# A hybrid diffusion backbone on one core: TensorE's instructions kept in the order of the source

## The chip, the cores and the metric

The kernel runs on one core of one Trainium2 chip. The metric is device time in microseconds (us), median of three runs. The engines of the core are TensorE (PE, matmuls and transposes; its weight loads are shown apart as PEld), VectorE (DVE), ScalarE (ACT), GpSimd (POOL) and SyncE (SP), which issues most DMA transfers. Every engine works through its own list of instructions in order and waits at the head of the list for semaphores of the others.

## The reference, cut to what matters

Two layers (DEPTH = 2) run over 1024 latent tokens and 128 context tokens, width 1024. Each layer has a modulated RMSNorm, three groups of mixers that share one input and one output projection, and a squared-ReLU MLP:

```python
h = rmsnorm(x, p['norm_mix_pre']) * (1 + scale1) + shift1
proj = h @ p['w_in']
o_a = block_attention(qa, k_all, v_all, HEAD_DIM ** -0.5)              # 6 heads, 2 of keys
o_b = block_attention(q_b, k_b, kv[..., B_NOPE:], (B_NOPE + B_ROPE) ** -0.5)  # 4 heads, low rank
o_c, h_fin = ssd_mixer(z, xbc, dt_raw, p, h0)                          # state-space scan, both ways
x = x + gate1 * rmsnorm(concatenate([o_a, o_b, o_c]) @ p['w_out'], p['norm_mix_post'])
h = rmsnorm(x, p['norm_ffn_pre']) * (1 + scale2) + shift2
f = square(relu(h @ p['w_ffn1'])) @ p['w_ffn2']
x = x + gate2 * rmsnorm(f, p['norm_ffn_post'])
```

Softmax in block_attention is over all 1152 keys for latent queries and over the 128 context keys for context queries.

## The kernel before, in words

The 1152 tokens are nine tiles of 128, or three blocks of 384 (`NB = 3`). A product in full precision is made of three matmuls: operands are split into a rounded part (ACT, `cp`) and the rest (DVE or POOL, `lo`). Stages follow each other for each layer: `in_proj` (input projection, convolution, and the scan's first half `ssm_a`), `mix` (keys and values, attention, the scan's second half `ssm_b`, output projection), `ffn` (MLP), whose last part overlaps the next layer's start.

The program is written as one list of calls in Python. Side work is written as generators that stand in a list `self.bg`. At fixed places of the main work the source calls `self.pull(ns)`, which steps the generators, so that their instructions land among those of the main work; a generator can yield a number of nanoseconds for which it wants to be left alone (`D`), and `PU` holds what each place in the main work counts for. So the source has an order of its own, written out by hand. A scheduler then builds the list of each engine: it takes the instructions by their order in the source as priority, runs a timeline of its own, and lets a later instruction go first when the earlier one's inputs or buffers are not there yet. It does so for all five engines.

Attention works on groups, one head of one block of 384 queries: 12 groups with the low-rank keys, then 18 with the others, a layer. For a group `score` makes scores S (PE), copies them to P with a running maximum (DVE, L777), and after the third piece of a row of 128 queries takes the exponential of the row of 1152 (ACT). `trans` transposes P (PE, tile pt), and splits it into ph (ACT) and pl (DVE); `prod` multiplies with the values (PE, tile oT). The main loop issues this for each of nine pieces of 128 keys, with the scores of the next group between:

```python
            ts = [trans(g, 0), trans(g, 1)]
            for j in range(nj):
                if j + 2 < nj:
                    ts.append(trans(g, j + 2))
                if nx and j < 9:
                    score(nx, j // 3, j % 3)
                prod(g, j, ts[j])
```

Three more places matter. `o_split` transposes attention's output (PE, tile m) into the operands of `out_proj` (PE, tile op, 8 x 24 matmuls a block); for the last block that is issued after attention, together with the norms `prenorm` of the first two blocks. A norm has two steps on PE (`stats`): sums over the partitions (tile st), then, after a short chain on DVE and POOL, a broadcast of the factors (tile rb). `chain` in `ffn` runs two such norms a block while the MLP ends. The start of the kernel does the same for the three blocks of the input.

Of the kernel before, what the change touches and what calls it, by code (L numbers as in the profile page):

```python
# [30 lines left out]
class Group:  # L31

    def __init__(self, b, prep, V, scale, dst, done, pull, after=None):
        self.b, self.prep, self.V, self.scale, self.dst, self.done = b, prep, V, scale, dst, done
        self.pull, self.after = pull, after


class Net:
    def __init__(self, tc, a, o):
        self.tc, self.nc, self.a, self.o = tc, tc.nc, a, o  # L40
        self.bg = []
        self.used = [0.0, 0.0, 0.0]
        self.credit = self.now = self.hold = 0.0
        self.build()


    def pool(self, name, side="left", space=None, bufs=1):
# [1575 lines left out]
```

## Time and profile before

| | |
|---|---|
| median of 3 runs | 3482.16 us (3480.79 to 3486.63) |
| profiled execution, its own time | 3485.52 us |
| its span, first to last instruction | 3483.7 us |
| mean granted clock of TensorE | 0.963 |
| PE, DVE, ACT, POOL busy | 93%, 65%, 45%, 39% |

Busy is the share of the span in which the engine had an instruction under way. PE's matmuls are pipelined, each of them overlaps the next, so its busy time is not time at its peak. [...]

### The profile page before, as it was taken

Reading aid. Unit: us, or ns where it says so; the run is one execution under the profiler, and the core shown is the slowest. Engines: PE = TensorE matmul, PEld = TensorE weight load, DVE = VectorE, ACT = ScalarE, POOL = GpSimd, SP = SyncE. Lnnn points to the kernel's source line nnn. Section 1 sums busy time; section 2 is a strip of 40 time slices with the busy share of each in tenths; the row PEclk is TensorE's granted clock in tenths of the full one; section 3 lists DMA queues with packets and bytes.
Section 4 is the critical chain, followed back from the end, with each engine's and each line's share of the span. In section 5 each row is a group of like instructions: output and inputs, shape, how many; then the busy total and the mean of one; then the engine's idle time right before and its main releaser. Section 6 shows DMA issues by size and latency. Waiting matters only on the chain. (4 is left out here: it accounts for less than half of the span.)

```text
span 3483.7 us, 50649 instructions
## 1 busy us (share of the span) xinstructions
PE 3234.2 (93%) x18578; PEld 3055.2 (88%) x18578; DVE 2257.0 (65%) x5318; ACT 1557.5 (45%) x3250; POOL 1348.8 (39%) x996
## 2 busy tenths in 40 slices
PE   6988799998899999999989887999888999999997
PEld 3966698788799999999989676989887999999997
DVE  6876888765647778774588767887658223333236
ACT  4464677665441221112454646787654411222223
POOL 6357432144651122113573673331356412111145
PEclk8989899999999999999999998999998999999999
DMA  5253333413332333322432533322233211111134
GB/s 212 80 175 104 115 86 116 164 49 97 126 103 80 94 99 98 91 91 73 145 120 97 170 112 111 89 92 67 79 108 98 85 37 45 41 43 43 37 97 145
DMA packets 164525, 340.71 MB, mean 98 GB/s; under 512 B 14429, under 2 KB 105909, under 8 KB 160693
## 3 DMA queue, kind: packets, MB, share of 16 engines
q1 hardware_dynamic: 161012, 335.32, 30.2%
q8 instruction: 146, 2.39, 0.3%
q10 hardware_dynamic: 3264, 2.16, 0.2%
q14 instruction: 103, 0.84, 0.1%
HBM read 280.99 MB, written 56.44 MB: 97 GB/s over the span
## 5 line engine op out<-in xcount | busy, mean ns | idle before, releaser
L78 POOL TENSOR_TENSOR w<-raw,w 128x1024 fp32r<-128x1024 f32 (+1 forms) x266 | 650.6, 2451 | 1370.8 <-ACT w L65 1314.8
L69 PE MATMUL g<-h,w 128*128 128x384 f32 x5328 | 971.5, 342 | 10.5 <-DVE h L78 6.4
L69 PEld LDWEIGHTS g<-h,w 128*128 128x128 f32 x5328 | 949.5, 190 | 16.5 <-DVE h L78 8.6
L69 PE MATMUL g<-big,w 128*128 128x384 f32 x4608 | 818.7, 336 | 8.4 <-DVE big L78 3.4
L69 PEld LDWEIGHTS g<-big,w 128*128 128x128 f32 x4608 | 802.5, 189 | 12.4 <-DVE big L78 5.2
L65 ACT CAST w<-raw 128x1024 fp32r<-128x1024 f32 (+1 forms) x266 | 275.9, 1042 | 643.5 <-PE g L69 353.1
L83 DVE TENSOR_TENSOR big<-big,g 128x384 f32<-128x384 f32 x336 | 181.8, 550 | 289.4 <-PE g L69 289.1
L83 DVE TENSOR_TENSOR r<-r 128x384 f32<-128x384 f32 x192 | 148.5, 773 | 329.0 <-ACT r L97 328.4
L69 PE MATMUL g<-w,h 128*128 128x512 f32 (+1 forms) x1296 | 321.6, 402 | 31.1 <-ACT w L65 12.2
L777 DVE TENSOR_SCALAR_CACHE_REDUCE P<-S 128x384 f32<-128x384 f32 (+1 forms) x500 | 265.8, 541 | 112.3 <-PE S L69 108.3
L69 PEld LDWEIGHTS g<-w,h 128*128 128x128 f32 x1296 | 252.7, 199 | 77.4 <-ACT w L65 13.5
L78 DVE TENSOR_TENSOR pl<-pt,ph 128x384 fp32r<-128x384 f32 (+2 forms) x560 | 267.7, 498 | 43.4 <-ACT ph L65 39.7
L65 ACT CAST ph<-pt 128x384 fp32r<-128x384 f32 (+2 forms) x560 | 232.2, 445 | 84.4 <-PE pt L73 72.1
L93 DVE SCALAR_TENSOR_TENSOR macc<-raw,cT,macc 128x128 f32<-128x128 f32 x784 | 259.9, 393 | 0.0
L73 PE MATMUL pt<-cst,P 128*128 128x128 f32 x1460 | 257.9, 276 | 0.5 <-DVE pl L78 0.3
L97 ACT ACTIVATE r<-g 128x384 f32<-128x384 f32 x192 | 94.2, 491 | 355.2 <-PE g L69 354.9
L78 DVE TENSOR_TENSOR big<-r,big 128x384 fp32r<-128x384 f32 x192 | 172.3, 897 | 92.6 <-ACT big L65 92.4
L69 PE MATMUL op<-big,w 128*128 128x384 f32 x1152 | 227.3, 340 | 2.0 <-DVE big L78 1.6
L97 ACT ACTIVATE P<-P,mx 128x1152 f32<-128x1152 f32 x180 | 210.4, 1170 | 37.0 <-DVE mx L89 36.0
L69 PEld LDWEIGHTS op<-big,w 128*128 128x128 f32 x1152 | 199.2, 188 | 3.2 <-DVE big L78 2.2
L73 PEld LDWEIGHTS pt<-cst,P 128*128 128x128 f32 x1460 | 189.3, 142 | 14.1 <-ACT P L97 0.9
L65 ACT CAST big<-r 128x384 fp32r<-128x384 f32 x192 | 98.4, 513 | 195.8 <-DVE r L83 195.6
(291 smaller groups left out, 4782.9 us busy)
## 6 DMA issues: line engine op xcount, KB each, us to landing
raw<-in_w SPq DMA_DIRECT2D x176, 512.0 KB, 3.5
raw<-in_w_mod SPq DMA_DIRECT2D x80, 512.0 KB, 3.7
raw<-in_w_out SPq DMA_DIRECT2D x48, 512.0 KB, 3.7
big<-s_x SPq DMA_DIRECT2D x13, 1536.0 KB
E<-s_ac SPq DMA_DIRECT2D x36, 384.0 KB, 4.4
s_x<-big SPq DMA_DIRECT2D x9, 1536.0 KB, 5.1
cv<-s_cv SPq DMA_DIRECT2D x36, 320.0 KB, 3.9
h<-in_w_mod SPq DMA_DIRECT2D x16, 512.0 KB, 9.9
```

The source lines that it names most:

```text
L65: self.nc.scalar.copy(out, in_)
L69: self.nc.tensor.matmul(out, lhsT=lhsT, rhs=rhs, start=start, stop=stop)
L73: self.nc.tensor.transpose(out, in_, self.ident[:p, :p])
L78: (eng or self.nc.vector).tensor_tensor(out=out, in0=src, in1=hi.bitcast(F32), op=ALU.subtract)
L83: (eng or self.nc.vector).tensor_tensor(out=out, in0=a, in1=b, op=op)
L93: self.nc.vector.scalar_tensor_tensor(out=out, in0=a, scalar=s, in1=b, op0=op0, op1=op1)
L97: self.nc.scalar.activation(out=out, in_=in_, func=func, **kw)
L777: nc.vector.tensor_scalar(out=p[:, j * 384:j * 384 + nk], in0=S, scalar1=1.0, scalar2=None, op0=ALU.mult, op1=ALU.max, accum_out=mx[:, j:j ...
```

## The change

The call of `build()`, which issues the whole program, is put into a block in which the scheduler leaves PE's instructions in the order in which the source issues them. The other engines, and the DMA queue of SyncE, are ordered by the scheduler as before.

```diff
@@ -41,7 +41,8 @@
         self.bg = []
         self.used = [0.0, 0.0, 0.0]
         self.credit = self.now = self.hold = 0.0
-        self.build()
+        with tc.manual_schedule(engines={mybir.EngineType.PE}):
+            self.build()
```

Line numbers below L42 are one higher in the changed kernel, and the numbers in buffer names two higher.

The first place is PE at the border between two groups of attention in layer 0. S_4140 (S_4142 in the changed kernel) is the last piece of scores of the third row P_4104 (P_4106) of a group. Before, 26 instructions stand between it and the first transpose of that row; the last of these rows are:

```order
L69 MATMUL S_4203<-KT_3357,qh_4085 128x384
L69 MATMUL S_4203<-KT_3357,ql_4086 128x384
L69 MATMUL S_4183<-KR_3519,qq_4093 128x384
L69 MATMUL S_4203<-KR_3519,qq_4093 128x384
L73 MATMUL m_4210<-cst_63,oS_4155 128x128 x3
L69 MATMUL S_4227<-KT_3357,qh_4085 128x384
L69 MATMUL S_4227<-KT_3357,ql_4086 128x384
L69 MATMUL S_4227<-KR_3519,qq_4093 128x384
L69 MATMUL S_4255<-KT_3357,qh_4085 128x384
L69 MATMUL S_4255<-KT_3357,ql_4086 128x384
L69 MATMUL S_4255<-KR_3519,qq_4093 128x384
L73 MATMUL pt_4157<-cst_63,P_4104 128x128
```

Here the scores of the following group stand ahead of that transpose, which is the last row. In the changed kernel PE has there, from the last piece of scores on:

```order
L70 MATMUL S_4142<-KT_3359,qh_3855 128x384
L70 MATMUL S_4142<-KT_3359,ql_3856 128x384
L70 MATMUL S_4142<-KR_3521,qq_3863 128x384
L70 MATMUL oT_3947<-ph_4102,V_3456 128x384
L70 MATMUL oT_3947<-pl_4103,V_3456 128x384
L74 MATMUL pt_4159<-cst_65,P_3940 128x128
L74 MATMUL pt_4159<-cst_65,P_4023 128x128
L74 MATMUL pt_4159<-cst_65,P_4106 128x128
L74 MATMUL pt_4167<-cst_65,P_3940 128x128
L74 MATMUL pt_4167<-cst_65,P_4023 128x128
L74 MATMUL pt_4167<-cst_65,P_4106 128x128
L74 MATMUL pt_4175<-cst_65,P_3940 128x128
```

Two products oT and two transposes stand now between the scores S_4142 and the first transpose of P_4106; the scores of the following group come behind all nine transposes.

The second place is PE between attention and the MLP of layer 0, where op is the output projection of the last block, and st and rb are the two steps of the norms of the first two blocks. Before, the broadcasts rb stood behind the last op:

```order
L69 MATMUL op_10596<-big_10200,w_10560 128x384
L69 MATMUL op_10596<-big_10199,w_10560 128x384 x2
L69 MATMUL op_10596<-big_10200,w_10560 128x384
L69 MATMUL op_10596<-big_10199,w_10560 128x384 x2
L69 MATMUL op_10596<-big_10200,w_10560 128x384
L69 MATMUL op_10596<-big_10199,w_10560 128x384
L69 MATMUL rb_10403<-h_10289,cst_63 128x384
L69 MATMUL g_10652<-h_10290,w_10633 128x384
L69 MATMUL g_10692<-h_10290,w_10633 128x384
L69 MATMUL g_10724<-h_10290,w_10643 128x384
L69 MATMUL g_10763<-h_10290,w_10643 128x384
L69 MATMUL rb_10419<-h_10298,cst_63 128x384
```

Before this, the matmuls of six op tiles stand mixed with the transposes of `o_split`. In the changed kernel PE has:

```order
L70 MATMUL op_10374<-big_10201,w_10366 128x384
L70 MATMUL st_10381<-cst_65,h_10291 128x2 x3
L70 MATMUL op_10374<-big_10201,w_10366 128x384
L70 MATMUL op_10374<-big_10202,w_10366 128x384
L70 MATMUL op_10374<-big_10201,w_10366 128x384
L70 MATMUL st_10393<-cst_65,h_10300 128x2 x3
L70 MATMUL op_10374<-big_10201,w_10366 128x384
L70 MATMUL op_10374<-big_10202,w_10366 128x384
L70 MATMUL op_10374<-big_10201,w_10366 128x384
L70 MATMUL rb_10405<-h_10291,cst_65 128x384
L70 MATMUL op_10374<-big_10201,w_10371 128x384
L70 MATMUL op_10374<-big_10202,w_10371 128x384
```

The first broadcast, rb_10405, stands now in the third of eight op tiles, and the second eight rows further on; all op matmuls stand behind the last transpose of `o_split`.

## Rows read from the trace of the kernel before

**Rows 1.** Page, part 1: busy us, share of the span, instructions.

```profile
PE 3234.2 (93%) x18578; PEld 3055.2 (88%) x18578; DVE 2257.0 (65%) x5318; ACT 1557.5 (45%) x3250; POOL 1348.8 (39%) x996
```

**Rows 2.** Table by stage: window, length, busy us (instructions), clock, DMA.

```profile
core 0: us, PE busy (x) PEld busy (x) DVE busy (x) ACT busy (x) POOL busy (x), PEclk, DMA share, GB/s
...
110.00:358.00 248.00, 219.99 (x1040) 190.65 (x1038) 177.23 (x366) 122.07 (x343) 138.04 (x165) 0.93 0.38 123
...
404.00:875.00 471.00, 446.77 (x2923) 402.31 (x2922) 353.68 (x1158) 332.88 (x736) 157.24 (x139) 0.97 0.32 100
875.00:966.00 91.00, 74.43 (x404) 70.33 (x405) 63.67 (x81) 43.55 (x70) 62.03 (x33) 0.91 0.38 131
...
1717.00:1855.00 138.00, 120.60 (x617) 115.56 (x616) 117.83 (x151) 65.04 (x113) 98.69 (x46) 0.91 0.40 137
...
2137.00:2583.00 446.00, 423.17 (x2784) 393.12 (x2782) 348.98 (x1148) 329.24 (x726) 158.38 (x139) 0.98 0.26 79
```

**Rows 3.** PE's waits over the span: total us, times, longest.

```profile
PE S L69 <- DVE P L777: 31.2, 23, 5.8
...
PE rb L69 <- DVE h L83: 18.0, 5, 5.8
PE st L69 <- DVE h L83: 15.3, 4, 7.4
...
PE pt L73 <- ACT P L97: 0.2, 1, 0.2
```

**Rows 4.** Chain that ended last: start us, us, what.

```profile
2695.31 704.95 PE g L69 x4028
```

**Rows 5.** Timeline, attention of layer 0, PE: start us, us, what.

```profile
465.05 0.71 PE L73 MATMUL pt<-cst,P 128*128 128x128 f32 x5
```

**Rows 6.** Timeline, attention of layer 0: a last score and its exponential.

```profile
740.41 0.33 PE L69 MATMUL S<-KY,ql 128*128 128x384 f32 x1
...
741.77 1.26 ACT L97 ACTIVATE P<-P,mx 128x1152 f32<-128x1152 f32 x1
```

**Rows 7.** Timeline, attention of layer 0: another last score and its exponential.

```profile
445.11 0.34 PE L69 MATMUL S<-KR,qq 128*128 128x384 f32 x1
...
448.03 1.26 ACT L97 ACTIVATE P<-P,mx 128x1152 f32<-128x1152 f32 x1
```

**Rows 8.** Table by stretch inside attention, columns as in group 2.

```profile
668.40:671.80 3.40, 3.40 (x14) 3.20 (x13) 1.68 (x8) 1.13 (x3) 3.40 (x2) 0.50 0.65 205
671.80:675.20 3.40, 3.16 (x21) 2.64 (x19) 3.04 (x12) 2.21 (x5) 0.61 (x1) 0.94 0.78 241
```

**Rows 9.** Timeline, PE, ahead of that stretch, with its idle time before.

```profile
666.66 1.01 PE L69 MATMUL S<-KY,ql 128*128 128x384 f32 x2 [2.09 <-DVE ql L78]
```

**Rows 10.** Timeline, PE, between attention and MLP of layer 0.

```profile
895.00 0.49 PE L73 MATMUL m<-cst,so 128*128 128x128 f32 x3
895.24 11.52 PE L69 MATMUL op<-big,w 128*128 128x384 f32 x65
...
912.70 3.73 PE L69 MATMUL op<-big,w 128*128 128x384 f32 x20
919.04 0.88 PE L69 MATMUL rb<-h,cst 128*128 128x384 f32 x2 [2.60 <-DVE h L83]
...
929.16 1.62 PE L69 MATMUL rb<-h,cst 128*128 128x384 f32 x2 [5.80 <-DVE h L83]
```

**Rows 11.** Timeline, PE, end of layer 0's MLP: the first block's norms.

```profile
1716.86 0.72 PE L69 MATMUL st<-cst,h 128*128 128x2 f32 x6
...
1724.24 0.81 PE L69 MATMUL rb<-h,cst 128*128 128x384 f32 x2
...
1746.78 0.80 PE L69 MATMUL st<-cst,h 128*128 128x2 f32 x6 [0.97 <-DVE h L83]
```

**Rows 12.** Timeline, PE, start of the kernel: the second block's norm.

```profile
67.16 0.83 PE L69 MATMUL st<-cst,sq 128*128 128x2 f32 x6 [0.94 <-DVE sq L83]
...
77.23 0.81 PE L69 MATMUL rb<-sq,cst 128*128 128x384 f32 x2
```

## The prediction, made before the changed kernel ran

> **What bounds the kernel now.** I read the page first: TensorE (PE) is busy 93% of the span, VectorE (DVE) 65% [rows 1]. A mean over stages can mislead, so the second view is the table by stage. In attention PE is busy 446.8 of 471 us in layer 0 and 423.2 of 446 in layer 1, and DVE 353.7 and 349.0: PE is the limit, with DVE close behind. In the stretch between attention and the MLP (875 to 966) PE is busy 74.4 of 91 us, in the stretch from the MLP of layer 0 into layer 1 (1717 to 1855) 120.6 of 138 with DVE at 117.8, and in the input projection 220.0 of 248 [rows 2]. Those stretches are not PE's alone. The MLP is: in the chain of waits one piece of 4028 matmuls in a row takes 704.95 us, 0.175 us each [rows 4]. The two orders hardly differ there, so that piece and the other layer's MLP between 966 and 1717, some 1,450 us of the span, are out of play. Third, PE's own waits: the largest, scores on DVE, is only 31.2 us in 23 waits, and the two norm steps (rb, st) are 18.0 and 15.3 [rows 3]. The order that the scheduler made therefore leaves PE little idle time. Whatever the new order makes PE wait for, it mostly pays.
>
> **The change, part by part.** No instruction is added or removed: PE has the same 18264 matmuls and transposes. In the program of before 980 of them have a higher number in the source than the one behind them; in the changed one none has. The other engines and the DMA queue (SyncE's) are still ordered by the scheduler, and keep running ahead as far as buffers allow. So the price is the waits at the head of PE's line: a PE instruction whose input is late now holds all later ones.
>
> *Group boundaries in attention.* Before, between the last score of a row of queries (S) and the first transpose of that row's probabilities (P), the scheduler put 26 instructions at the place shown in the change's section; in the source's order there are two oT products and two transposes. A product or score spaces at 0.175 us [rows 4]; five transposes take 0.71 us of which one alone is 0.27, so they space at (0.71-0.27)/4 = 0.11 [rows 5]. The cover is 2 x 0.17 + 2 x 0.11 = 0.56 us. What must happen meanwhile is: DVE copies the score with a maximum, two short DVE operations, then ScalarE's exponential over 1152 columns. The shortest case in the trace ends 743.03 - 740.74 = 2.29 us after the last score (741.77 + 1.26 against 740.41 + 0.33), and one in the middle of the field 449.29 - 445.45 = 3.84 us [rows 6, 7]. At such a boundary the last steps have no more casts of transposes for DVE, so I take a value nearer the short end, 2.6 us. I counted all 180 rows of P in the new order: 21 have the cover of 0.56 us, 25 more have less than 2.6 us (output-projection matmuls or small transposes between). 21 x 2.04 + 25 x 0.95 = 67 us. Bounds: 53 us with the 2.29 us chain, 135 us with 3.84 (62 places).
>
> *TensorE's clock after such waits.* [...] What PE did before it fell: it waited 2.09 us up to 666.66 for a query's low half [rows 9]. [...]
>
> *Output-transposes and queries inside attention.* The output of attention is transposed in three blocks of 24 transposes a layer, and each new group brings three to six transposes of queries; each waits for a copy and a subtraction that free its PSUM buffer, or for a query as in [rows 9]. Most have a whole step of matmuls ahead of them; I take 8 us, four waits of 2.09. Bounds: 0, and 30 us with some 14 of them.
>
> *Between attention and MLP.* Before, the last transposes of the output (m<-so) run at 895.0, and of 192 output-projection matmuls only 103 come after them (three rows, the first with 65 and the last with 20); 89 had run ahead in the gaps, on six open accumulators [rows 10]. In the new order all 192 stand behind that transpose: 89 x 0.175 = 15.6 us come later. In addition both norm broadcasts (rb, 919.0 and 929.2) stood behind the last of those matmuls and now stand in their midst, after 60 and 69 of them, with 123 matmuls (22 us) behind. PE gets there at 895.2 + 0.175 x 60 = 906 and waits for DVE until about 919 and 929. Then 22 us of projection: it ends near 951 in place of 912.7 + 3.7 = 916. Part is given back: before, PE waited 5.80 us for the second rb after that, and DVE works off the normalised input meanwhile. I take 20 us a layer, 40 in all; bounds 0 and 35 a layer.
>
> *MLP of layer 0 into layer 1.* Each of three blocks has two norms in a row. In before, st to rb takes 1724.2 - 1716.9 = 7.4 us and rb to the next st 22.5 us [rows 11], with other matmuls between. In the new order 12 and 60 matmuls (2.1 and 10.5 us) stand between, so up to 5 and 12 us of each pair are exposed, 52 us for three. Against that, PE is idle for 17.4 us there already and DVE needs its 117.8 us in any order [rows 2]; the exposed time is time in which DVE is not disturbed. I take 20 us; bounds 0 and 40.
>
> *Start.* st at 67.2 and rb at 77.2 [rows 12] have 6 matmuls between them in the new order, where the scheduler had put three token tiles' worth. Twice such a norm, about 8 us exposed each: 15 us; bounds 0 and 20.
>
> *Input projection.* The pieces of the state-space scan are pulled in by hand between projection matmuls. Before, PE ran those matmuls early and the scan's transposes late; now each late one holds the projection. PE's 28 us of slack in 248 [rows 2] shows that the scan sets part of that stretch. I take 8 us a layer, 16; bounds 0 and 25 a layer.
>
> Sum: 67 + 40 + 8 + 40 + 20 + 15 + 16 = 206 us. The profiled execution took 3485.5 us, 1.8 more than its span; 3485.5 + 206 = 3691.5. The median of the three timed runs is 3.4 us lower, so I give **3690 us**.
>
> **The rivals.**
> *The waits fall into slack that is there already.* PE's busy time may flatter it: in attention its weight loads are busy 402.3 of 471 and 393.1 of 446 us [rows 2], 122 us less than the stages. If that slack takes up the waits of attention, the first three terms vanish: 206 - 115 = 91, so 3573 us. [...] Against it: at 0.175 and 0.11 us a piece the spacing of the attention matmuls fills nearly all of PE's busy time, so the slack is not free at the boundaries.
> *The clock swings at every boundary.* [...] For it: after one wait of 2.09 us the clock fell [rows 8, 9]. Against it: in before 23 waits of scores on DVE [rows 3] left attention at a mean clock of 0.97 and 0.98 [rows 2].
> *Faster.* The scheduler places by times of its own, and where it is wrong, an instruction that it moved ahead holds PE. If the waits of scores on DVE and the norm steps come from such moves and the source's places are late enough, 31.2 + 18.0 + 15.3 = 64.5 us go, and the time is 3418 us. It decides where the cover at a boundary is as long as the chain; 0.56 against 2.29 us speaks against it.
> *The change does nothing.* The rows of the order exclude it outside the MLP; only waits that cancel could give it.
>
> **How the numbers follow.** Waits paid as above, 3600 to 3860 us: 0.72. Absorbed in attention, 3500 to 3600: 0.12. Clock swings, over 3860: 0.08. Faster: 0.05. Within 0.2% (7 us, what a measurement of this kernel can tell from no change): 0.03. The range 3550 to 3860 leaves out the upper rival, half of the absorbed case's lower part, and the last two. Faster 0.05, same 0.03, slower 0.92.
>
> **What would show it.** Right: PE's waits of transposes for the exponential (pt on ACT's P) grow from 0.2 us [rows 3] to some 50 us or more in about 46 places; attention loses 50 us or more a layer; the stretch to the MLP is some 20 us longer; the MLP takes what it took; DVE's busy share falls. Wrong: PE's wait list stays led by scores on DVE with some 30 us, or attention keeps its length; then the first term fell. If the granted clock in attention stays at 0.97, the second did.

## The result, and the profile after

The changed kernel takes 3796.98 us (median of 4 runs, 3795.37 to 3800.53) against 3481.47 us of the kernel before on the same chips: ratio 1.0906, 95% interval 1.0887 to 1.0925, 315 us more. The forecast was 3690 us with a range from 3550 to 3860. Direction, range and the main mechanism held; the sum of 206 us was a third too small.

The page's first part, as in [rows 1]: PE has the same 18578 instructions and 87 us more busy time, in a span that is 313 us longer. So 226 us are new idle time of PE. (The 18264 of the prediction counts the program's instructions, and no trace shows that number.)

```profile
PE 3320.8 (87%) x18578; PEld 3112.3 (82%) x18578; DVE 2288.0 (60%) x5318; ACT 1574.9 (41%) x3250; POOL 1344.6 (35%) x996
```

The table by stage answers to [rows 2] (window, length, busy us with instructions, granted clock as a share of full speed, DMA). The stretches are now cut where PE's stages really begin and end, so the lengths compare with the list below it, not one to one with those windows.

```profile
427.20:980.90 553.70, 470.06 (x2942) 416.17 (x2940) 371.50 (x1174) 342.73 (x744) 161.04 (x142) 0.95 0.27 88
...
1842.00:2053.00 211.00, 165.04 (x783) 153.82 (x782) 137.92 (x197) 84.36 (x155) 107.68 (x52) 0.85 0.29 100
...
2329.00:2861.90 532.90, 450.66 (x2798) 408.56 (x2796) 369.38 (x1154) 338.59 (x732) 161.32 (x142) 0.95 0.22 68
```

Attention of layer 0 in the kernel before, cut at the same instructions ([rows 2] has it from 404 to 875):

```profile
398.00:873.50 475.50, 451.65 (x2940) 406.79 (x2940) 358.28 (x1174) 335.83 (x740) 159.66 (x142) 0.97 0.33 103
```

By the start of the first PE instruction of each stage (first k, first S, last oT, first product with the second MLP matrix, first projection of layer 1), read in the timelines of both kernels, the 312.8 us divide so:

| stretch, us | before | after | difference | in the sum |
|---|---|---|---|---|
| start and input projection, layer 0 | 367.8 | 399.5 | +31.7 | 15 + 8 |
| keys and values, both layers | 59.5 | 54.9 | -4.6 | 0 |
| attention, layer 0 | 475.5 | 553.7 | +78.2 | 57.5 |
| attention, layer 1 | 449.8 | 533.0 | +83.2 | 57.5 |
| attention to MLP, both layers | 194.4 | 210.2 | +15.8 | 40 |
| MLP of layer 0, up to layer 1 | 822.6 | 879.6 | +57.0 | 20 |
| input projection, layer 1 | 310.9 | 336.0 | +25.1 | 8 |
| MLP of layer 1, to the end | 803.2 | 829.6 | +26.4 | 0 |

PE's waits over the span (total us, times, longest) answer to [rows 3]. The list is led by the wait that the prediction named: transposes of P for the exponential, 57.1 us in 40 places, from 0.2 us in one. The old leader, scores on DVE, fell from 31.2 us in 23 waits to 2.7 us in 7.

```profile
PE pt L74 <- ACT P L98: 57.1, 40, 3.9
...
PE oT L70 <- DVE pl L79: 28.0, 32, 5.5
...
PE oT L70 <- ACT ph L66: 16.0, 16, 3.0
...
PE S L70 <- DVE P L778: 2.7, 7, 0.7
```

One boundary between groups in the timeline of attention, layer 0 (start us, us, what, in square brackets the idle time before it and what ended it). It is the pattern of the change's section: the last score (S), two products, two transposes, and then the third row's transpose, which PE waits for.

```profile
469.45 0.42 PE L70 MATMUL S<-KT,qh 128*128 128x384 f32 x1
469.71 0.34 PE L70 MATMUL S<-KT,ql 128*128 128x384 f32 x1
469.88 0.34 PE L70 MATMUL S<-KR,qq 128*128 128x384 f32 x1
470.06 0.34 PE L70 MATMUL oT<-ph,V 128*128 128x384 f32 x1
470.24 0.34 PE L70 MATMUL oT<-pl,V 128*128 128x384 f32 x1
470.41 0.38 PE L74 MATMUL pt<-cst,P 128*128 128x128 f32 x2
473.00 1.39 PE L74 MATMUL pt<-cst,P 128*128 128x128 f32 x7 [2.21 <-ACT P L98]
474.05 0.67 PE L70 MATMUL S<-KT,qh 128*128 128x384 f32 x1
474.51 0.52 PE L70 MATMUL S<-KT,ql 128*128 128x384 f32 x1
...
471.60 1.25 ACT L98 ACTIVATE P<-P,mx 128x1152 f32<-128x1152 f32 x1 [0.52 <-DVE mx L90]
```

From the end of the last score (470.22) to the end of the exponential (471.60 + 1.25 = 472.85) are 2.6 us, the value taken in the forecast. Behind the wait the second score follows the first by 0.46 us (474.05 to 474.51), where it had 0.26 just before it (469.45 to 469.71). The stretches ahead of the wait, in it, behind it and after that go with this: the granted clock is 1.00, in the wait too, then 0.56 for 3.9 us, near the 0.50 of [rows 8], then 1.00 again.

```profile
465.00:470.40 5.40, 4.86 (x32) 4.56 (x32) 4.74 (x15) 5.30 (x14) 0.06 (x1) 1.00 0.18 50
470.40:473.00 2.60, 0.39 (x3) 0.14 (x1) 1.15 (x6) 2.04 (x4) 0.77 (x1) 1.00 0.50 129
473.00:476.90 3.90, 3.90 (x17) 3.80 (x18) 2.22 (x6) 1.66 (x4) 0.00 (x0) 0.56 0.00 0
476.90:480.00 3.10, 3.10 (x23) 3.03 (x22) 2.48 (x8) 1.49 (x4) 0.51 (x1) 1.00 0.00 0
```

### The profile page after: what moved, and what is told of

It is laid out like the page before. It is cut to its first block, busy times and chain, and to the rows that moved or that the text cites. A ratio compares the mean times of both kernels' runs of the same rounds, so it can differ in the third digit from the quotient of the medians.

```text
span 3796.5 us, 50535 instructions
## 1 busy us (share of the span) xinstructions
PE 3320.8 (87%) x18578; PEld 3112.3 (82%) x18578; DVE 2288.0 (60%) x5318; ACT 1574.9 (41%) x3250; POOL 1344.6 (35%) x996
## 5 line engine op out<-in xcount | busy, mean ns | idle before, releaser
L70 PE MATMUL g<-big,w 128*128 128x384 f32 x4608 | 838.9, 341 | 33.5 <-DVE big L79 19.9
L70 PEld LDWEIGHTS g<-big,w 128*128 128x128 f32 x4608 | 814.8, 191 | 45.0 <-DVE big L79 24.8
L70 PE MATMUL g<-w,h 128*128 128x512 f32 (+1 forms) x1296 | 331.0, 409 | 16.0 <-DVE big L84 5.5
L74 PE MATMUL pt<-cst,P 128*128 128x128 f32 x1460 | 257.8, 288 | 57.2 <-ACT P L98 57.1
```

The source lines that it names most:

```text
L70: self.nc.tensor.matmul(out, lhsT=lhsT, rhs=rhs, start=start, stop=stop)
L74: self.nc.tensor.transpose(out, in_, self.ident[:p, :p])
```

## The experiments

Theory: each PE instruction whose input is late holds all behind it, stretch by stretch, and the losses add up. In attention the largest are the boundaries between groups. Rivals: the order acts as one chain, so that a stretch only inherits or passes on delay; and, for attention, VectorE sets the pace and the boundary is only where it shows. All runs are of the whole kernel.

**Attention alone, and all but attention.** In the first, only the attention loop of the kernel before is kept in source order; the second is the changed kernel with that loop given back to the scheduler.

```diff
-        self.attn(groups, at, ps)
+        with self.tc.manual_schedule(engines={mybir.EngineType.PE}):
+            self.attn(groups, at, ps)
```

> The kernel before, with PE kept in the order of the source in the attention loop alone, in both layers. Theory (each stretch pays its own waits at the head of PE's line, whatever stands around it): the loss is what attention lost in the changed kernel, 78 + 82 = 160 us, so about 3640 us (3615 to 3670), PE's waits of pt on ACT's P between 45 and 65 us, and PE's clock in attention 0.95. Rival (attention only inherits lateness from the input projection and the norms ahead of it, which fill the other engines' lists): under 3560 us.

> The complement: the changed kernel with the attention loop given back to the scheduler. Theory (local, additive): 3797 - 160 = 3637 us (3610 to 3665); no waits of pt on ACT's P above 3 us in sum; attention is 476 and 450 us long again. Rival (the order is one chain, and PE pays the same later elsewhere): above 3700 us.

Measured: 3650.94 us (ratio 1.0467, 1.0452 to 1.0483) and 3640.65 us (1.0438, 1.0420 to 1.0455), against 3486.01 us of the kernel before beside them. The two losses, 164.9 and 154.6 us, add to 319.5; the whole change costs 315.5. PE's waits in the first kernel, and the window of layer 0's attention in the first and in the second (which has no wait of pt for ACT's P in its list):

```profile
PE pt L73 <- ACT P L97: 59.3, 43, 3.9
```

```profile
395.90:952.00 556.10, 470.68 (x2940) 416.74 (x2940) 371.12 (x1174) 342.30 (x741) 161.97 (x144) 0.95 0.28 88
```

```profile
423.60:907.50 483.90, 456.82 (x2940) 412.17 (x2940) 361.69 (x1176) 338.30 (x742) 160.51 (x144) 0.96 0.32 101
```

The waits of pt come and go with the order of that loop, whatever stands around it. Attention kept alone in source order is as long (556.1 and 540.8 us) as in the changed kernel or longer; given back alone it takes 483.9 and 455.3 us, 8.4 and 5.5 more than before, where its old length was expected. The rivals of an inherited or a passed-on delay fall. About half of the cost is attention's, half lies outside.

**Moving the boundary in the source.** Three kernels with PE in source order throughout, each with one edit more. First the scores of the next group earlier; then also its first two transposes in the last two steps of a group; then also the scores from two steps before the group's end on.

```diff
-                    score(nx, j // 3, j % 3)
+                    for s in ((0, 1), (2, 3), (4, 5), (6,), (7,), (8,))[j] if j < 6 else ():
+                        score(nx, s // 3, s % 3)
```

```diff
-            ts = [trans(g, 0), trans(g, 1)]
+            ts = ahead or [trans(g, 0), trans(g, 1)]
+            ahead = []
             for j in range(nj):
                 if j + 2 < nj:
                     ts.append(trans(g, j + 2))
+                elif nx:
+                    ahead.append(trans(nx, j + 2 - nj))
```

```diff
-                if nx and j < 9:
-                    for s in ((0, 1), (2, 3), (4, 5), (6,), (7,), (8,))[j] if j < 6 else ():
-                        score(nx, s // 3, s % 3)
+                if nx and j < 5:
+                    score(nx, (j + 4) // 3, (j + 4) % 3)
+                if n + 2 < ng and j in (7, 8):
+                    for s in (2 * j - 14, 2 * j - 13):
+                        score(groups[n + 2], s // 3, s % 3)
```

> The changed kernel with one edit of the source's order: the nine scores of the next group are issued in the first six steps of a group (two a step, then one) in place of nine, so that the last stands three steps ahead of the boundary. Theory (the boundary waits for the chain score, maximum, exponential): the waits of pt on ACT's P fall from 57 to under 15 us and some of the lost clock comes back; the first oT product of a group still waits for its cast and subtraction (59 us of oT waits stay): 3797 - 45 - 20 = about 3730 us (3700 to 3750). Rival (DVE sets attention's pace, and the wait only shows at the boundary): scores in pairs wait for DVE's copies instead (S on DVE's P up from under 10 to over 40 us), and the time is 3780 to 3810 us.

> The changed kernel with the early scores of e3 and a second edit: the first two transposes of the next group are issued in the last two steps of a group, so that their casts and subtractions run under its last products. Theory: the oT waits of a group's first product (59 us) go too, the clock in attention returns to 0.97, and attention is within 15 us of its old length in each layer: 3797 - 160 + 20 = about 3655 us (3630 to 3685). Rival (DVE sets attention's pace): no more than 30 us below the run with early scores alone.

> The run with pipelined groups, where the scores of the group after next now begin in the last two steps of a group, two a step, and the last score of a group stands three steps ahead of its first transpose instead of two. Theory (what is left there, 31 us of pt waiting for ACT's P and 20 of oT on casts, is the length of the chain again, since the transposes moved two steps towards the scores): both fall under 15 us together, and attention comes within 20 us of its old length in each layer: 3757 - 60 = about 3695 us (3670 to 3715). Rival (VectorE's list, as the scheduler put it, is late for other reasons, and moving PE's scores only moves the wait): above 3735 us, with S waiting for DVE's P in place of pt.

Measured: 3759.4 (3755.7 to 3762.8), 3756.9 (3747.5 to 3758.3) and 3733.8 us (3724.8 to 3734.9), so 38, 40 and 63 us below the changed kernel where 67, 142 and 102 were expected. All three times lie outside the range of their theory. The second came out as its rival had it, no more than 30 us below the first (2.5 us); the third, 3733.8 us, is just under its rival's 3735. PE's waits in the three, in that order:

```profile
PE oT L70 <- DVE pl L79: 23.6, 35, 5.5
...
PE S L70 <- DVE P L778: 14.3, 30, 3.7
...
PE pt L74 <- ACT P L98: 5.3, 4, 2.1
```

```profile
PE pt L74 <- ACT P L98: 31.0, 26, 3.1
```

```profile
PE oT L70 <- DVE pl L79: 25.6, 13, 6.4
...
PE pt L74 <- ACT P L98: 16.5, 16, 1.3
```

The first edit did to its wait what was expected (57.1 to 5.3 us), and S took up 11.6 us, far from the 40 of the rival. The difference, 40 us, is the time that it won. Clock and busy time did not come back (0.94 and 0.96 in the two attention windows, after 0.95 in both; PE busy there 473.0 and 451.5 us, after 470.1 and 450.7), and the waits of oT stayed, as the expectation said. The second edit brought the pt waits back (31.0), because it moved the transposes two steps towards the scores. The third mended that in part. Summed over all releasers in the two attention windows, PE waits: before 52 us (S 41, oT 7, m 4), after 164 (oT 62, pt 57, m 31, S 3, others 10), last kernel 111 (oT 41, m 32, pt 17, S 10, others 12). So the theory's mechanism holds for pt and its sizes don't: with the boundary moved, the waits of oT and of the side work's transposes (m) stay, and attention is still 39 and 54 us longer than before. The replacement wait that the rivals named, S on DVE, did not come in their size either (14.3 us in the first, 10 in the last). So VectorE's pace is not shown as the bound of attention, and is not excluded by these three runs; the kernels without side work, below, speak against it for a part of the loop. Where the waits of oT stand is told with the prediction.

**The same source order under the scheduler.** The second of these edits, without the change.

> The kernel before (PE ordered by the scheduler) with the early scores and the early transposes of the run with pipelined groups. Theory (the scheduler undoes what the source's order does badly, and had little idle time to give): within 15 us of 3481 us. Rival (the source's order is a better guide than the one written by hand, also for the scheduler): 3465 us or less.

Measured: 3482.98 us, ratio 0.9999 (0.9989 to 1.0009). What is worth 40 us to a PE that follows the source is worth nothing to one that the scheduler orders.

**The loop without its side work.** `self.pull(g.pull)` is taken out of the attention loop, in the kernel before and in the changed one; the side work comes in a lump where it is needed.

> The kernel before with no side work pulled into the attention loop: the pieces of the scan and of the two output stages are issued in a lump at the places that need them, so that the first ten of the twelve low-rank groups of a layer are the attention loop and its queries alone. Its whole time says little; it is the reference for its twin with PE in the order of the source. Both theories: about 13 us a group in that stretch, PE idle under 5%.

> The same with PE in the order of the source. Attention lost 160 us over 60 groups, 2.7 us a group. Theory (the waits at the group boundaries, with the first product behind them, make it nearly all): a group takes 2.2 us or more longer than in the twin. Rival (the side work's own waits, pieces of the scan and of the output that hold the loop, make about half, as the 63 us suggest that the run with earlier scores won back by moving the boundary alone): 1.0 to 1.7 us longer.

Measured: 3655.34 and 3983.79 us. The stretch from the first product of the second group to that of the eleventh, in layer 0, with the scheduler and with the source's order:

```profile
421.00:522.60 101.60, 101.36 (x697) 96.42 (x696) 90.83 (x319) 83.11 (x192) 4.57 (x9) 1.00 0.08 24
```

```profile
453.80:580.00 126.20, 110.37 (x697) 102.04 (x697) 97.03 (x321) 86.23 (x192) 4.57 (x9) 0.96 0.06 20
```

And PE's waits in that stretch of the latter, with one of those of oT in the timeline:

```profile
PE pt L74 <- ACT P L98: 9.6, 6, 1.6
PE oT L70 <- DVE pl L79: 3.8, 9, 0.5
...
464.70 0.45 PE L70 MATMUL oT<-pl,V 128*128 128x384 f32 x1 [0.51 <-DVE pl L79]
```

The same 697 PE instructions take 24.6 us longer: 2.7 us a group over nine groups, as the theory said (2.2 or more), not 1.0 to 1.7. (The scheduled twin takes 11.3 us a group where 13 were expected, idle under 5% as expected.) 15.6 us more are idle (pt, and oT for its cast and subtraction), 9.0 more busy at a clock of 0.96. One thing is not as the theory had it: oT waits at the last products of a group, ahead of the boundary, and not at the first product behind it. VectorE is busy 90.8 of 101.6 us and 97.0 of 126.2, so it has more idle time in the longer stretch and does not set the pace there. With side work the same stretch takes 126.9 us before and 161.9 after in layer 0, and 126.9 and 156.5 in layer 1. If the loop's own waits cost the same with side work, 24.6 of 35.0 and of 29.6 us, 70 to 83%, are its group boundaries. That holds for nine of a layer's 29 boundaries; for the others there is no such pair. Their whole times show a second thing: placing the side work by hand is worth 171 us to the scheduled kernel too (3655.3 against 3484.6). The scheduler did not make up for source order of that coarseness.

**Filling the wait.** Eight transposes of a constant ahead of the waiting one.

```diff
+                if j == 0 and i == rw[-1]:
+                    for _ in range(FILL):
+                        self.tr(pt[:, i * 128:i * 128 + 128], self.cst[:, 1, :])
```

> The changed kernel with eight transposes of a constant (128 columns, 0.11 us each) put ahead of the transpose that waits at a group boundary; the real transposes overwrite them. They do 0.9 us of work in a place where PE waits 1.4 us in 40 of the 60 cases, and delay the other 20 by up to 0.9 us (18 us in all). Theory (the waits at the boundaries pull the clock down, and half of the 42 us by which attention's busy time grew is clock): the granted clock in attention rises from 0.95 to 0.96 or 0.97, which gives back 10 to 20 us, and the time is 3785 to 3805 us. Rival (the clock falls for other stretches, not for these waits): the clock stays at 0.95 or below and the time is 3810 us or more.

Measured: 3797.64 us (3795.5 to 3801.5), the time of the changed kernel with 480 instructions more. The boundary shown above in this kernel (timeline), and its attention window of layer 0:

```profile
470.21 1.04 PE L75 MATMUL pt<-cst 128*128 128x128 f32 x8
472.61 0.98 PE L75 MATMUL pt<-cst,P 128*128 128x128 f32 x7 [1.36 <-ACT P L99]
473.34 0.42 PE L71 MATMUL S<-KT,qh 128*128 128x384 f32 x1
473.60 0.34 PE L71 MATMUL S<-KT,ql 128*128 128x384 f32 x1
```

```profile
427.80:981.90 554.10, 490.58 (x3182) 437.17 (x3180) 371.32 (x1174) 343.04 (x744) 161.73 (x142) 0.96 0.27 88
```

With the wait filled, the scores behind it keep their full pace (0.26 us from the first to the second, not 0.46); without it they ran at a granted clock of 0.56 for 3.9 us. The clock of attention goes from 0.95 to 0.96 in both layers, and over nine groups of layer 0 from 0.94 (458.4 to 620.3) to 0.98 (here 458 to 616), so the waits do pull it down, as the theory had it. They are not all that does: with the scores earlier, pt waited only 5.3 us, and the clock of the two attention windows was 0.94 and 0.96. The waits of pt fall by 30.6 us, to 26.5. The filling itself takes 480 x 0.11 = 53 us of PE, an estimate; PE's busy time in attention grew by 37 us (490.6 and 467.2 after 470.1 and 450.7), so some 16 us came back in pace. It is an estimate, not a measurement of the clock alone, and the whole time stays as it was.

**The layer's ends, and the MLP.** The first is the changed kernel with PE given back to the scheduler from the last eighth of each MLP into the next layer's projections (up to `need(2)`); the second the kernel before, with the source's order only around the loop over the first seven eighths of the MLP.

```diff
+        self.man(False)
         self.drain()
         chains = []
```

```diff
-        for c in range(7):
+        with self.tc.manual_schedule(engines={mybir.EngineType.PE}):
+            for c in range(7):
```

> The changed kernel with PE given back to the scheduler from the last eighth of each layer's MLP (its two norms a block) through the first projections of the next layer, up to where the queue of that layer's first token tiles ends. Theory (the pairs of norm steps st and rb with too few matmuls between them cost 44 us at the MLP's end of layer 0 and 24 us at the end of the kernel): 3797 - 68 = about 3729 us (3710 to 3745), and the stretch from the MLP into layer 1 takes the 166 us of before again in place of 211. Rival (the stretch is set by VectorE, busy 138 us in either kernel, and by what the earlier MLP left over): above 3770 us.

> The kernel before, with PE kept in the order of the source only in the first seven eighths of the MLP of both layers. Theory (the 28 us that the MLP lost, which the prediction put at nothing, come from its own order: the first product on a new activation or accumulator stands right behind the one that makes it): 3481 + 28 = about 3510 us (3495 to 3520). Rival (the MLP's first block only inherits the lateness of the norms ahead of it): within 7 us of before.

Measured: 3732.75 us (3728.1 to 3737.5) and 3509.74 us (ratio 1.0066, 1.0051 to 1.0082). The first gives back 64 us, as the theory had it: the MLP of layer 0 up to layer 1 takes 842.4 us in place of 879.6, the input projection behind it 328.1 in place of 336.0, the MLP of layer 1 to the end 804.8 in place of 829.6. Against the kernel before, layer 0's MLP is still 20 us longer; that is what its first seven eighths lost, which stay in source order (735.4 us before, 756.0 in the changed kernel, 755.0 here). The timeline of PE there in the changed kernel, and with the ends given back; they answer to [rows 11]:

```profile
1885.84 1.16 PE L70 MATMUL rb<-h,cst 128*128 128x384 f32 x2
...
1915.37 1.41 PE L70 MATMUL st<-cst,h 128*128 128x2 f32 x6 [9.50 <-DVE h L84]
```

```profile
1863.59 0.81 PE L78 MATMUL rb<-h,cst 128*128 128x384 f32 x2
...
1886.11 0.80 PE L78 MATMUL st<-cst,h 128*128 128x2 f32 x6 [0.95 <-DVE h L92]
```

From rb to the st of the second norm of a block there are 29.5 us with 9.50 of waiting in the source's order, and 22.5 with 0.95 under the scheduler.

The second costs 25.5 us, within its expectation, but only partly where it said. The first seven eighths take 15 us more in layer 0 (750.4 for 735.4) and 2.5 in layer 1 (711.0 for 708.5), and the part behind them is shorter again: the stretches from the MLP's first product to layer 1 and to the end are 10.8 and 1.6 us longer; the rest is spread over layer 1's attention (+4.1) and other stretches, and is not explained. In the changed kernel the waits of the first seven eighths are of this kind (timeline of PE, layer 0):

```profile
1144.91 16.76 PE L70 MATMUL g<-big,w 128*128 128x384 f32 x86 [1.64 <-DVE big L79]
...
1272.51 9.75 PE L70 MATMUL g<-h,w 128*128 128x384 f32 x46 [1.92 <-POOL w L79]
```

The first product on a new activation (big) stands right behind the matmuls that make it, and waits 1.6 us for the subtraction of its rest; others wait 1.1 to 1.9 us for the split of a weight (w) on POOL.

**The one stretch that got shorter.** Only the making of keys and values ahead of attention is kept in the source's order.

```diff
+        with self.tc.manual_schedule(engines={mybir.EngineType.PE}):
+            ckvT = xb.tile([128, 2, 1280], R, name="ckvT")
...
```

> The kernel before, with PE kept in the order of the source only while keys and values of the low-rank part are made (the tiles k), ahead of attention. In the changed kernel that stretch took 27.7 and 27.2 us from the first k to the first S, in place of 30.2 and 29.3. Theory (here the scheduler's order is worse than the source's): 4 to 6 us faster, 3476 to 3480 us. Rival (what the scheduler loses there it has pulled ahead from attention, which then starts later): within 3 us of before.

Measured: 3479.29 us (12 runs) against 3484.57 (17 runs), ratio 0.9983, interval 0.9972 to 0.9993. It is the only version clearly faster than the kernel before, by 5 us or 0.17%, just under the 0.2% taken as the bound of a measurement at the start. The window of that stretch in layer 0:

```profile
367.70:395.70 28.00, 16.34 (x99) 15.58 (x98) 21.03 (x48) 14.98 (x39) 9.80 (x18) 0.79 0.23 72
```

It is 2.2 us shorter in layer 0 (28.0 for 30.2) and 0.2 in layer 1 (29.1 for 29.3); the other 4 us of the spans' difference are scattered over later stretches at 0.2 to 1.4 us each. That the order of these rows makes the gain is shown for less than half of it.

## Why the prediction was right, and where its sum was short

- *PE is the bound, and new waits at the head of its line are mostly paid.* Right: 226 us of new idle time and 87 of busy time make the 313 us, and the two complementary kernels show that the costs add.
- *Group boundaries, 67 us.* Right in place and size: pt waits for the exponential 57.1 us in 40 places (forecast: 46). The pair without side work confirms the boundary as the main cost of the loop where it was tried.
- *Clock, 40 us.* No run shows the 40 us that the sum holds for it. What the runs showed in its place: PE's busy time in attention grew by 18.4 and 23.7 us, 42 in all. Only about half is clock, by an estimate: cut at the same instructions, PE was busy 451.7 and 426.9 us before at a clock of 0.97, and at 0.95 after; that is 451.7 x (0.97/0.95 - 1) = 9.5 us in layer 0 and 9.0 in layer 1. For the other half a second estimate: PE's idle gaps in attention grew from 28 and 31 to 83 and 89, and a matmul that starts after a gap takes 0.34 us where the next ones add 0.175; 113 gaps more x 0.17 = 19 us. That 40 met 42 is luck: the sum held one of the two things that make the 42, at twice its size. [rows 8] was read too simply as well: cut more finely, the clock before was 1.00 up to 665.4 and 0.50 from there, so it fell within the wait of 2.09 us that ended at 666.66 [rows 9], and not behind it.
- *The step that failed in attention*: the sum looked for waits of transposes and queries, and held no term for the products, which wait for the cast and the subtraction of a transposed piece. The waits of oT grew from 7 to 62 us in the attention windows, 55 us that no term held. By their place in the timeline, 34 us are one product in the sixth piece of the 23rd group and one in the first piece of the 29th, with the matmul ahead of each, in both layers, where VectorE and ScalarE were at other work (last section). 18 us in 28 places stand at the last product of a group, ahead of the boundary, as the row at 464.70 above; only 8 us in 13 places stand at other first products, behind late transposes. So it is not an echo of the wait of pt: with the scores earlier that one fell to 5.3 us, and oT still waited 60, mostly in the same places. Against it stand 38 us that the sum did not give back: the waits of S, 41 us before, nearly vanish (3 us). That a PE which is late for its transposes is no longer early for its scores would explain it, and is not shown.
- *Queries and output transposes, 8 us*: under-sized; the waits of m grew from 4 to 31 us, inside the bound of 30.
- *Attention to MLP, 40 us*: over-sized, 15.8 measured. The broadcasts came into the midst of the projection as forecast, but did not wait there for DVE: the first ran without a wait, because the st step ahead of it had waited already. The timeline of PE, which answers to [rows 10]:

```profile
1014.48 1.41 PE L70 MATMUL st<-cst,h 128*128 128x2 f32 x6 [5.44 <-DVE st_v L90]
...
1016.86 1.48 PE L70 MATMUL rb<-h,cst 128*128 128x384 f32 x2
...
1020.71 19.53 PE L70 MATMUL op<-big,w 128*128 128x384 f32 x110
```

- *MLP into layer 1, 20 us, and the MLP at nothing*: this step failed most. 57 us for both in layer 0, and 26 in layer 1, where the sum had nothing. The prediction saw the pairs of norms and then put only 20 of 52 us, on the argument that DVE's 118 us bound that stretch; cut at the same instructions DVE was busy 139 us in 166 before and 138 in 211 after, so the stretch grew while DVE's work did not. For layer 1 it did not ask what the same norms do at the kernel's end. And "the two orders hardly differ" in the MLP was true of the rows and not of the time: a few of them, moved by a few places, wait 1 to 2 us each.
- *Start and input projection, 15 + 16 us*: 57 measured with layer 1's; inside the bounds (20 + 50).
- *Rivals.* Absorbed in attention: no. PE's weight loads, 406.8 us busy before in a stretch of 475.5, rose to 416.2 in 553.7, and nothing was absorbed: the new waits did not fit into the time that the loads left. The clock did not swing at every boundary (0.95 in the mean in either layer's attention, some 19 us there by the estimate above; that rival lay over 3860 us), and nothing got faster but the keys and values.

## What to carry to other kernels

An order of instructions that looks idle-free in the source has to be judged by the chain from the last instruction that feeds a late engine to the first one that needs its answer: here 2.6 us of VectorE and ScalarE against 0.56 us of cover, and the wait was paid in 40 places, with some of the clock on top (0.97 before and 0.95 after in attention). When such waits are counted, count every kind of instruction that stands behind its input with as little cover, and not only the one that looks worst: here the products waited as long as the transposes. Ask also which old waits vanish. Where a scheduler and an order by hand are compared, do it stretch by stretch, since they add: nearly all of them were better scheduled, one was not.

## What the runs showed of the hardware that was not expected

Two waits of oT a layer are not the group boundary's. In the changed kernel PE waits 7.46 us at 852.7 us and 5.53 us at 963.3 for DVE, and as long in layer 1 (7.5 and 5.5). The timelines of PE, DVE, and POOL beside them:

```profile
852.73 0.69 PE L70 MATMUL oT<-pl,VY 128*128 128x384 f32 x1 [7.46 <-DVE mx L783]
...
963.29 0.58 PE L70 MATMUL oT<-pl,VY 128*128 128x256 f32 x1 [5.53 <-DVE pl L79]
...
842.10 6.69 DVE L90 TENSOR_SCALAR big<-big,der 128x384 f32<-128x384 f32 x4
...
849.18 2.55 DVE L90 TENSOR_SCALAR big<-big,der 128x384 f32<-128x384 f32 x2
...
855.86 0.75 DVE L90 TENSOR_SCALAR big<-big,der 128x384 f32<-128x384 f32 x2
...
955.06 7.83 DVE L90 TENSOR_SCALAR big<-big,der 128x384 f32<-128x384 f32 x4
...
842.43 3.73 POOL L84 TENSOR_TENSOR big<-big 128x768 f32<-128x768 f32 x2 [1.92 <-ACT big L98]
846.11 2.46 POOL L79 TENSOR_TENSOR w<-raw,w 128x1024 fp32r<-128x1024 f32 x1
848.53 2.99 POOL L84 TENSOR_TENSOR big<-big 128x768 f32<-128x768 f32 x2
```

The same scaling of 128 x 384 takes 1.3 us and more each while POOL is at work on tensors (here until 851.5), and 0.75 us for two of them once POOL is idle. What PE needs stands behind six of them at 852.7 and behind four at 963.3. Over the whole trace of the changed kernel, the 33 scalings of this shape that ran with no such work on POOL took 0.40 to 0.48 us each; of the 42 that ran beside it for over half of their time, 34 took 1.1 to 2.6 us and the other 8 at most 0.52. In the kernel before they range from 0.41 to 2.50 us too. No run here took POOL's work away, and the 8 fast ones are not explained, so that POOL's work is the cause is only argued.

The second is the clock: after a wait of 2.21 us, with 1.00 granted until then, PE ran at 0.56 for 3.9 us, and with 0.9 us of work put into the same wait (1.36 us left) it did not fall there: 1.00 from 469.36 to 483.21, a stretch with that wait in it.
